# Token mixing of a hybrid layer: products of two heads side by side, TensorE's order by hand, two mLSTM blocks ahead of the attention queries

## The chip, the cores and the metric

The kernel runs on one core of one Trainium2 chip. The metric is the device time of one execution in microseconds (us), the median of three runs. A core has five engines, each with its own list of instructions in a fixed order: TensorE (PE: matrix products and transposes; PEld is its loading of weights), VectorE (DVE), ScalarE (ACT), GpSimd (POOL) and SyncE (SP, which issues transfers). They meet through semaphores.

## What is computed

One decoder layer in fp32 on 512 tokens of width 1024: token mixing, cross attention into 256 memory tokens, and a PEER feed-forward part (512 tokens x 8 heads x 16 experts, each a row of a table of 16384). The change touches only the token mixing:

```
proj = rmsnorm(h) @ w_in                      # -> mq, mk, mv, mo, mi, mf, aq, ak, av
# mLSTM, 4 heads, keys of 64, values of 128, in chunks; per head and chunk:
s    = (q k^T) * d                            # d: decays from the gates mi, mf, causal
num  = s v + w_inter * (C q);   den = sum(s) + w_inter * (n . q)
h    = num / max(|den|, exp(-m));  C = decay * C + sum(w v k^T);  n = decay * n + sum(w k)
hm   = sigmoid(mo) * rmsnorm_per_head(h)
# attention, 8 query heads on 2 key/value heads of 64, window 128, a sink logit per head:
p    = exp(scores - mx);  probs = p / (sum(p) + exp(sink - mx));  ha = probs @ av
h    = h + concat(hm, ha) @ w_out
```

## The kernel before

**Tiles.** The tokens stand in four blocks of 128 (`NB`). Dense products are made in three fp32r passes of a split operand: `whi`/`xhi` hold the value rounded to fp32r, `wlo`/`xlo` the rest, and each step is hi·hi, lo·hi, hi·lo (lines 946 to 948 with the weights on the stationary side, accumulator `acc_f`; lines 959 to 961 with the tokens stationary, accumulators `acc_o`, `acc_t`). The weights come as raw halves of 1 MB; ScalarE rounds them to `whi` and VectorE subtracts for `wlo` (lines 933 and 934, `load_w`, in as many pieces as `parts` says). `split_psum` does the same for results (lines 881 and 882). The small products of the mixing stage are plain fp32.

**Two shapes of small product use half of the array.** A product over the 64 channels of a head reads rows 0 to 63 or 64 to 127 ("64*128" in the trace): the mLSTM's `st` (line 212), the carried part of `num` (`num<-cst,qk`, line 253) and the scores `sp` (line 300). A product that makes 64 outputs fills columns 0 to 63 or 64 to 127 ("128*64"): `ds` (line 267, the update of the state `cst`) and `o_att` (line 334, the attention's output). An fp32 product stands in the trace as two records.

**Order of the stage, `front`.** After the dense projections of keys, values and gates, a loop over the four mLSTM heads makes `ab`, its exponential `dt` and `st`, and `pt` = `st` x `dt`. `wb` scales the queries in `qk`. The projection of the attention queries follows (`aq`, `acc_f0` to `acc_f3`, 96 passes). Then the string `MIX` interleaves three kinds of step over the blocks: `m` (a whole mLSTM block: keys `kw`, `num` of two tiles by row half, `den`, `hm`, the state update `ds`, the norm `rst`, four transposes `tp_hm` and their split), `s` (attention: scores of one half of the heads and their softmax, twice; then the transposes `tp_p`, the copies `pT` and the output of one half, twice) and `x` (the first 512 columns of `w_out` for one block, 24 `acc_o` products, and the residual). The softmax is eight exponentials on ScalarE per block (line 310) and scalings shared by VectorE (line 319) and ScalarE (line 317). The second half of `w_out` (`mix_out`) comes after the stage.

**What sets the order.** The string is only the order in which the program is traced. A scheduler with its own estimate of times then orders each engine's list, and moves instructions where it thinks that an operand is ready. Tiles of PSUM come in tags: `a` with two buffers, `b` with four, `d` with two; scores and output products share `b`, `num`, `st` and `ds` share `d`, transposes have `a`. A transfer of 8 MB of zeros (`wd<-zero`) is issued after `aq` is evacuated, and the loads of `w_out`'s first half are issued there too.

Of the kernel before, what the change touches and what calls it, by code (L numbers as in the profile page):

```python
# [21 lines left out]
P = 128  # L22
# [36 lines left out]
MIX = "s0 s1 m0 s0 s0 m1 s0 x0 s1 s2 s1 s1 s2 m2 s3 s2 s2 m3 s3 x1 x2 s3 s3 x3"  # L59
# [15 lines left out]
def front(c):  # L75
# [125 lines left out]
    for h in range(4):  # L201
        ab = ps.tile([P, 512], F32, tag="d", name="ab")
        T.matmul(ab, c.sel[:, h], raf, start=True, stop=False)
        T.matmul(ab, c.identb, c.cmask, start=False, stop=True)
        dt = c.np_.tile([P, D], F32, tag="xs", bufs=4, name="dt")[:, :S]
        for b in range(NB):
            A.activation(dt[:, b * P:(b + 1) * P], ab[:, b * P:(b + 1) * P], AF.Exp, bias=cols[:, b, h:h + 1])
# [14 lines left out]
    aq = fp.tile([P, 4, S], F32, name="aq")  # L222

    def evac_aq(j, acc):
        c.act_aq = A.copy(aq[:, j], acc)

    gemm_fm(c, [a["w_in_m"][3, hf] for hf in range(2)], evac_aq)

# [9 lines left out]
    hss = fp.tile([P, NB, 4], F32, name="hss")  # L238
    junk = fp.tile([P, P], F32, name="junk_h")
    def mlstm(b):  # L240
        t = slice(b * P, (b + 1) * P)
        hm = fp.tile([P, 4, P], F32, tag="hm", bufs=2, name="hm")
        if b < NB - 1:
            kw = make_kw(b)
        for hh in range(2):
            num = ps.tile([P, 512], F32, tag="d", name="num")
            n3 = num[:, :258].rearrange("p (h d) -> p h d", h=2)
            r = slice(64 * hh, 64 * hh + 64)
            for pr in range(2):
                h = 2 * pr + hh  # L250
                T.matmul(n3[:, pr], pt[h][:, t], vx[:, b, h], start=True, stop=(b == 0))
                if b:
                    T.matmul(n3[:, pr], qk[r, pr, t], cst[r, pr], start=False, stop=True)
            den = fp.tile([P, 2], F32, tag="den", bufs=2, name="den")
            A.activation(den, n3[:, :, P], AF.Abs)
            V.tensor_tensor(den, den, cols[:, b, 64 + hh:68 + hh:2], op=ALU.max)
            V.reciprocal(den, den)
            for pr in range(2):
                h = 2 * pr + hh
                V.tensor_scalar(hm[:, h], n3[:, pr, :P], den[:, pr:pr + 1], None, op0=ALU.mult)  # L260
                A.activation(junk, hm[:, h], AF.Square, accum_out=hss[:, b, h:h + 1])
        if b < NB - 1:
# [20 lines left out]
    def swa(b):  # L283
# [5 lines left out]
        scs = []  # L289
        for g in range(2):  # L290
            r = slice(64 * g, 64 * g + 64)
            snk = c.sinks[:, 4 * g:4 * g + 4]
            sc = fp.tile([P, 4, 256], F32, tag="sc", bufs=3, name="sc")
            mx = fp.tile([P, 4], F32, tag="mx", bufs=2, name="mx")
            for jj in range(2):
                sp = ps.tile([P, 512], F32, tag="b", name="sp")
                for j2 in range(2):
                    j = 2 * jj + j2
                    sl = sp[:, j2 * 256:j2 * 256 + nk]
                    T.matmul(sl, aq[r, j, t], kT[r, k0:k0 + nk], start=True, stop=True)  # L300
                    V.tensor_tensor_reduce(sc[:, j, :nk], sl, msk, 1.0, FMIN,
                                           op0=ALU.add, op1=ALU.max, accum_out=mx[:, j:j + 1])
            nm = fp.tile([P, 4], F32, tag="nm", bufs=2, name="nm")
            V.scalar_tensor_tensor(mx, mx, 0.125, snk, op0=ALU.mult, op1=ALU.max)
            V.tensor_scalar(nm, mx, -1.0, None, op0=ALU.mult)
            es = fp.tile([P, 4], F32, tag="es", bufs=2, name="es")
            V.tensor_tensor(es, snk, mx, op=ALU.subtract)
            den = fp.tile([P, 4], F32, tag="den4", bufs=2, name="den4")
            for j in range(4):
                A.activation(sc[:, j, :nk], sc[:, j, :nk], AF.Exp, bias=nm[:, j:j + 1], scale=0.125,  # L310
                             accum_out=den[:, j:j + 1])
            A.activation(es, es, AF.Exp)
            V.tensor_tensor(den, den, es, op=ALU.add)
            V.reciprocal(den, den)
            for j in range(4):
                if j % 2:
                    A.activation(sc[:, j, :nk], sc[:, j, :nk], AF.Copy, scale=den[:, j:j + 1])
                else:
                    V.tensor_scalar(sc[:, j, :nk], sc[:, j, :nk], den[:, j:j + 1], None, op0=ALU.mult)
            scs.append(sc)  # L320
            yield
        o = ps.tile([P, 512], F32, tag="b", name="o_att")
        for g, sc in enumerate(scs):
            pT = c.np_.tile([P, D], F32, tag="xs", bufs=4, name="pT")
            for kk in range(nkt):
                tp = ps.tile([P, 512], F32, tag="a", name="tp_p")
                for j in range(4):
                    T.transpose(tp[:, j * P:(j + 1) * P], sc[:, j, kk * P:(kk + 1) * P], ident)
                if kk:
                    A.copy(pT[:, 512:1024], tp)  # L330
                else:
                    V.tensor_copy(pT[:, 0:512], tp)
            for kk in range(nkt):
                T.matmul(o[64 * g:64 * g + 64], av[:, k0 // P + kk, 64 * g:64 * g + 64],  # L334
                         pT[:, kk * 512:(kk + 1) * 512], start=(kk == 0), stop=(kk == nkt - 1))
            if g == 0:
                yield
        split_psum(c, c.xhi[:, 4:8, t], c.xlo[:, 4:8, t], o.rearrange("p (h t) -> p h t", h=4))

# [6 lines left out]
    wo = [load_w(c, a["w_out"][0, hf], 512) for hf in range(2)]  # L346

    def mix0(b):
        acc = ps.tile([P, 512], F32, tag="b", name="acc_o")
        for hf in range(2):  # L350
            mm3_tm(c, acc, wo[hf], slice(0, 512), hf, b)
# [864 lines left out]
```

## Time and profile before

| | us |
|---|---|
| median of three runs | 1676.47 (1675.79 to 1678.25) |
| the profiled execution, its own time | 1678.69 |
| its span in the trace | 1676.9 |
| TensorE busy in the span | 1638.2 (98%) |
| VectorE busy | 1227.4 (73%) |
| ScalarE busy | 722.5 (43%) |
| TensorE's granted clock, mean | 0.986 |

The span is the time between the first and the last instruction of the profiled execution; the 1.8 us beside it are the start and the end of the run. A view by stages gives, for each stretch, how long each engine was busy and how many instructions it ran, the clock granted to TensorE as a share of full speed, and the load of the transfers. In a timeline, a row is a run of like instructions with its start; the start of the next row tells what the first one costs TensorE, since the records of products overlap (a record's length reaches into the next). The mixing stage lies between about 102 and 219 us of the span; the dense projection of the attention queries ends at 136.2 us.

### The profile page before, as it was taken

The numbers are of one execution on the slowest core, as the hardware profiler recorded it, in microseconds if no ns is written. First come the engines' busy times: TensorE is split into PE (matmuls) and PEld (weight loads), VectorE is DVE, ScalarE is ACT, GpSimd is POOL, SyncE is SP. The second block draws the span as 40 slices with busy tenths as digits, with TensorE's granted clock in tenths as the row PEclk, the third lists the DMA queues.
The fourth block names the chain that finished last, engine by engine and source line by source line (L and its number), as shares of the span: only waits on it lengthen the run. The fifth ranks groups of instructions, "written<-read, shape, count | busy, mean of one in ns | idle before, by whom it ended". The sixth has DMA issues, their size and how long they took to land.

```text
span 1676.9 us, 22996 instructions
## 1 busy us (share of the span) xinstructions
PE 1638.2 (98%) x8368; PEld 1427.2 (85%) x8368; DVE 1227.4 (73%) x2701; ACT 722.5 (43%) x1206; POOL 601.7 (36%) x427
## 2 busy tenths in 40 slices
PE   7999999999999999999999999999999999999987
PEld 5776579878999999899998988888888888888765
DVE  5535556465597888877887778878778888887985
ACT  5434544353354445578753333333333333333323
POOL 2000000000007878887423344434444344443620
PEclk9997999999999999999999999999999999999999
DMA  6236025215145444677999989898899899887992
GB/s 212 74 129 248 15 99 189 101 68 212 70 139 145 120 114 101 171 184 212 360 319 401 358 335 348 325 356 322 325 350 374 294 351 358 342 325 256 394 358 100
DMA packets 149105, 400.58 MB, mean 239 GB/s; under 512 B 28144, under 2 KB 62080, under 8 KB 136320
## 3 DMA queue, kind: packets, MB, share of 16 engines
q1 hardware_dynamic: 89232, 255.76, 41.6%
q0 software_dynamic: 55360, 134.32, 24.1%
q10 hardware_dynamic: 4400, 9.04, 1.5%
q8 instruction: 65, 1.06, 0.3%
q14 instruction: 48, 0.39, 0.1%
HBM read 356.28 MB, written 42.80 MB: 238 GB/s over the span
## 4 chain that ended last, share of the span: by engine, by line
PE 92%; DVE 3%; DMA 2%; issue 2%; ACT 1%; SPq 0%; DVEq 0%; POOLq 0%; POOL 0%; ACTq 0%
PE acc_d L782 10%; PE acc_d L780 10%; PE acc_d L781 10%; PE acc_u L847 9%; PE acc_u L846 9%; PE acc_u L848 9%; PE acc_f L946 4%; PE acc_f L948 4%; PE acc_f L947 4%; PE w L686 3%; PE acc_t L959 2%; PE acc_t L961 2%; PE acc_t L960 2%; PE sp L300 1%; PE o_att L334 1%
## 5 line engine op out<-in xcount | busy, mean ns | idle before, releaser
L780 PE MATMUL acc_d<-xhi,dh 128*128 128x384 f32 x1024 | 351.0, 343 | 4.6 <-ACT dh L731 3.6
L782 PE MATMUL acc_d<-xhi,dl 128*128 128x384 f32 x1024 | 345.7, 338 | 1.3 <-DVE dl L769 1.3
L781 PE MATMUL acc_d<-xlo,dh 128*128 128x384 f32 x1024 | 344.8, 337 | 0.0
L847 PE MATMUL acc_u<-ul,ch 128*128 128x512 f32 x762 | 299.2, 393 | 2.3 <-DVE ul L825 2.3
L848 PE MATMUL acc_u<-uh,cl 128*128 128x512 f32 x762 | 298.4, 392 | 0.0
L631 POOL DMA_INDIRECT wd<-gg,ei x128 | 234.4, 1831 | 148.4 <-DVE ei L625 87.3
L708 POOL DMA_INDIRECT rows<-in_down_r_dram,eidx x128 | 167.5, 1309 | 253.2 <-DVE dots L714 235.9
L708 POOL DMA_INDIRECT rows<-in_up_dram,eidx x128 | 175.5, 1371 | 214.3 <-DVE gacc L724 189.5
L834 ACT CAST ch<-cf 128x384 fp32r<-128x384 f32 x127 | 65.2, 514 | 395.1 <-issue 213.9
L846 PE MATMUL acc_u<-uh,ch 128*128 128x512 f32 x762 | 217.2, 392 | 3.6 <-ACT uh L731 3.6
L769 DVE TENSOR_TENSOR dl<-draw,dh 128x1024 fp32r<-128x1024 f32 x128 | 156.3, 1222 | 80.7 <-ACT dh L731 77.6
L731 ACT CAST dh<-draw 128x1024 fp32r<-128x1024 f32 x128 | 133.9, 1049 | 160.6 <-PE acc_d L781 137.0
L780 PEld LDWEIGHTS acc_d<-xhi,dh 128*128 128x128 f32 x1024 | 193.9, 189 | 9.5 <-ACT dh L731 3.9
L782 PEld LDWEIGHTS acc_d<-xhi,dl 128*128 128x128 f32 x1024 | 193.5, 189 | 5.5 <-DVE dl L769 2.4
L781 PEld LDWEIGHTS acc_d<-xlo,dh 128*128 128x128 f32 x1024 | 193.7, 189 | 4.0
L847 PEld LDWEIGHTS acc_u<-ul,ch 128*128 128x128 f32 x762 | 143.5, 188 | 33.8 <-DVE ul L825 4.8
L846 PEld LDWEIGHTS acc_u<-uh,ch 128*128 128x128 f32 x762 | 142.1, 188 | 31.0 <-ACT uh L731 4.5
L848 PEld LDWEIGHTS acc_u<-uh,cl 128*128 128x128 f32 x762 | 143.6, 188 | 28.7
L724 DVE SCALAR_TENSOR_TENSOR gacc<-rows,coef,gacc 128x1024 f32<-128x1024 f32 x127 | 162.8, 1282 | 0.4
L825 DVE TENSOR_TENSOR ul<-uraw,uh 128x1024 fp32r<-128x1024 f32 x127 | 154.7, 1223 | 2.9 <-ACT uh L731 2.1
L714 DVE CUSTOM_DVE_ANT_0 rows<-rows,xn 128x1024 f32<-128x1024 f32 x128 | 154.8, 1221 | 0.0
L835 DVE TENSOR_TENSOR cl<-cf,ch 128x384 fp32r<-128x384 f32 x127 | 70.7, 557 | 113.7 <-ACT ch L834 113.6
(333 smaller groups left out, 2667.6 us busy)
## 6 DMA issues: line engine op xcount, KB each, us to landing
draw<-in_down_t_dram SPq DMA_DIRECT2D x64, 1024.0 KB, 7.2
uraw<-in_up_dram SPq DMA_DIRECT2D x64, 1024.0 KB, 8.1
wt<-wd SPq DMA_DIRECT2D x96, 256.0 KB, 8.6
wd<-stg SPq DMA_DIRECT2D x8, 2048.0 KB, 11.8
gd<-gsp SPq DMA_DIRECT2D x17, 768.0 KB, 4.0
gsr<-gd SPq DMA_DIRECT2D x17, 768.0 KB, 10.6
wd<-zero ACTq DMA_DIRECT2D x1, 8192.0 KB, 27.7
raw<-in_w_pq_dram SPq DMA_DIRECT2D x8, 1024.0 KB, 5.3
```

The costliest lines, as they stand in the source:

```text
L631: i = G.indirect_dma_start(out=out, out_offset=bass.IndirectOffsetOnAxis(ap=ei[:, h, k:k + 1], axis=0), in_=c.gg[:, NG, hh, k:k + 1], in_o ...
L708: G.indirect_dma_start(out=r, out_offset=None, in_=src, in_offset=bass.IndirectOffsetOnAxis(ap=c.eidx[:, j:j + 1], axis=0))
L714: V.tensor_tensor_reduce(r, r, c.xn0, 1.0, 0.0, op0=ALU.mult, op1=ALU.add, accum_out=dots[:, j:j + 1])
L724: V.scalar_tensor_tensor(c.gacc, r, coef[:, j:j + 1], c.gacc, op0=ALU.mult, op1=ALU.add)
L769: c.dl = nc.vector.tensor_tensor(self.lo, raw, f32(self.hi), op=ALU.subtract)
L780: T.matmul(acc[:, :TD], self.hi[:, ks], c.xhi[:, k, NG * P:], start=(k == 0), stop=False)
L781: T.matmul(acc[:, :TD], self.hi[:, ks], c.xlo[:, k, NG * P:], start=False, stop=False)
L782: T.matmul(acc[:, :TD], self.lo[:, ks], c.xhi[:, k, NG * P:], start=False, stop=(k == KT - 1))
L825: V.tensor_tensor(lo, raw, f32(hi), op=ALU.subtract)
L846: T.matmul(acc[b][n], ch[:, t], hi[:, d], start=st, stop=False)
L847: T.matmul(acc[b][n], ch[:, t], lo[:, d], start=False, stop=False)
L848: T.matmul(acc[b][n], cl[:, t], hi[:, d], start=False, stop=sp)
```

## The change

Products that use different halves of the array stand next to each other in TensorE's list, one of each half: `st` of two heads, `num` of the two row halves, scores of the two key/value heads, `o_att` of the two column halves. For that the softmax takes all eight heads of a block at once (`sc` is 128 x 8 x 256, two buffers instead of three of half the size). An mLSTM block is a generator of two steps, `num` to `rst` and then the update of the state; its transposes and split are a third step of their own, `n` (`mlstm_out`), and `tp_hm` takes a buffer of tag `d`, `st` one of `a`. `hm` has three buffers. The first two mLSTM blocks are traced ahead of the projection of `aq`. `x` has two steps of 12 products. The first half of `w_out` is loaded in four parts each. The scheduler may no longer move TensorE's instructions of the loop: they stand as traced (`manual_schedule`); the other engines are still ordered by the scheduler.

```diff
-MIX = "s0 s1 m0 s0 s0 m1 s0 x0 s1 s2 s1 s1 s2 m2 s3 s2 s2 m3 s3 x1 x2 s3 s3 x3"
+MIX = ("s0 s0 n0 n1 s1 m2 s1 x0 s0 m2 s0 x1 x0 s2 s1 s2 s1 s3 m3 s1 s3 n2 x1 x2 s2 n3 s2 x3 s2 s3 x2 s3 s3 x3")
...
-        st = ps.tile([P, 512], F32, tag="d", name="st")
-        r = slice(64 * (h % 2), 64 * (h % 2) + 64)
+        sts = [ps.tile([P, 512], F32, tag="a", name="st") for _ in range(2)]
         for b in range(NB):
             t = slice(b * P, (b + 1) * P)
-            T.matmul(st[:, t], qk[r, 2 + h // 2, t], qk[r, h // 2, t], start=True, stop=True)
+            for hh in range(2):
+                r = slice(64 * hh, 64 * hh + 64)
+                T.matmul(sts[hh][:, t], qk[r, 2 + pr, t], qk[r, pr, t], start=True, stop=True)
...
-        hm = fp.tile([P, 4, P], F32, tag="hm", bufs=2, name="hm")
+        hm = hms[b] = fp.tile([P, 4, P], F32, tag="hm", bufs=3, name="hm")
...
+        for pr in range(2):
+            for hh in range(2):
+                T.matmul(n3[hh][:, pr], pt[2 * pr + hh][:, t], vx[:, b, 2 * pr + hh], start=True, stop=(b == 0))
+            for hh in range(2):
+                if b:
+                    r = slice(64 * hh, 64 * hh + 64)
+                    T.matmul(n3[hh][:, pr], qk[r, pr, t], cst[r, pr], start=False, stop=True)
...
+        rsqrt(c, rst[:, b], hss[:, b], 1.0 / P)
+        yield
         if b < NB - 1:
             for pr in range(2):
                 ds = ps.tile([P, 512], F32, tag="d", name="ds")
...
+    def mlstm_out(b):
+        t = slice(b * P, (b + 1) * P)
+        hm = hms.pop(b)
+        tp = ps.tile([P, 512], F32, tag="d", name="tp_hm")
...
+        sc = fp.tile([P, 8, 256], F32, tag="sc", bufs=2, name="sc")
+        mx = fp.tile([P, 8], F32, tag="mx", bufs=2, name="mx")
+        for jj in range(2):
+
+            sps = [ps.tile([P, 512], F32, tag="b", name="sp") for _ in gs]
+            for j2 in range(2):
+                for g, r in enumerate(gs):
+                    T.matmul(sps[g][:, j2 * 256:j2 * 256 + nk], aq[r, 2 * jj + j2, t], kT[r, k0:k0 + nk],
+                             start=True, stop=True)
...
+        for kk in range(nkt):
+            for g, r in enumerate(gs):
+                T.matmul(o[r], av[:, k0 // P + kk, r], pT[g][:, kk * 512:(kk + 1) * 512],
+                         start=(kk == 0), stop=(kk == nkt - 1))
...
+    ml = [mlstm(b) for b in range(NB)]
+    for b in range(2):
+        step(ml[b], 2)
+    aq = fp.tile([P, 4, S], F32, name="aq")
...
-    wo = [load_w(c, a["w_out"][0, hf], 512) for hf in range(2)]
+    wo = [load_w(c, a["w_out"][0, hf], 512, parts=4) for hf in range(2)]
...
+    with tc.manual_schedule(engines={mybir.EngineType.PE}):
+        for op in MIX.split():
+            k, b = op[0], int(op[1])
+            if k == "n":
+                mlstm_out(b)
+            else:
+                step(it[k][b], 1)
```

TensorE's list at the end of the `aq` projection, before (the names are output<-operands, with buffer numbers, and the columns of the result):

```order
L947 MATMUL acc_f3_844<-xlo_89,whi_900 128x512
L948 MATMUL acc_f3_844<-xhi_88,wlo_901 128x512
L300 MATMUL sp_979<-kT_346,aq_840 128x128
L233 MATMUL tp_k_1037<-ident_71,qk_499 128x128 x2
L219 MATMUL wb_836<-wi_472,selp_233 128x512
L251 MATMUL num_1041<-vx_235,pt0_784 128x129
L251 MATMUL num_1041<-vx_235,pt2_814 128x129
L300 MATMUL sp_984<-kT_346,aq_840 128x128
```

The same place in TensorE's list after:

```order
L970 MATMUL acc_f3_930<-xhi_88,whi_932 128x512
L233 MATMUL tp_k_846<-ident_71,qk_499 128x128 x2
L971 MATMUL acc_f3_930<-xlo_89,whi_932 128x512
L233 MATMUL tp_k_885<-ident_71,qk_499 128x128 x2
L972 MATMUL acc_f3_930<-xhi_88,wlo_933 128x512
L252 MATMUL num_850<-vx_235,pt0_797 128x129
L252 MATMUL num_850<-vx_235,pt2_827 128x129
L970 MATMUL acc_f3_930<-xhi_88,whi_932 128x512
```

The key transposes of mLSTM blocks 0 and 1 and block 0's `num`, which stood behind the projection among the first scores, stand inside it.

TensorE's list around block 2's `num`, before:

```order
L300 MATMUL sp_1217<-kT_346,aq_840 128x256
L300 MATMUL sp_1222<-kT_346,aq_840 128x256
L251 MATMUL num_1341<-vx_235,pt0_784 128x129
L253 MATMUL num_1341<-cst_957,qk_499 128x129
L251 MATMUL num_1341<-vx_235,pt2_814 128x129
L253 MATMUL num_1341<-cst_957,qk_499 128x129
L251 MATMUL num_1354<-vx_235,pt1_799 128x129
L253 MATMUL num_1354<-cst_957,qk_499 128x129
L251 MATMUL num_1354<-vx_235,pt3_829 128x129
L253 MATMUL num_1354<-cst_957,qk_499 128x129
L334 MATMUL o_att_1115<-pT_1179,av_347 64x512
```

The same block's `num` after (line 252 is the full-row part, line 256 the half-row part, line 305 the scores):

```order
L233 MATMUL tp_k_1163<-ident_71,qk_499 128x128 x2
L252 MATMUL num_1167<-vx_235,pt0_797 128x129
L252 MATMUL num_1168<-vx_235,pt1_799 128x129
L256 MATMUL num_1167<-cst_840,qk_499 128x129
L256 MATMUL num_1168<-cst_840,qk_499 128x129
L252 MATMUL num_1167<-vx_235,pt2_827 128x129
L252 MATMUL num_1168<-vx_235,pt3_829 128x129
L256 MATMUL num_1167<-cst_840,qk_499 128x129
L256 MATMUL num_1168<-cst_840,qk_499 128x129
L305 MATMUL sp_1196<-kT_346,aq_926 128x256
L305 MATMUL sp_1197<-kT_346,aq_926 128x256
```

Full-row and half-row products alternated one by one; now two of the one shape are followed by two of the other, and the two half-row products, as the two scores behind them, read different rows.

ScalarE's list between two blocks' softmax, before (line 310 is an exponential, line 330 a copy of `pT`, line 261 a square of the mLSTM's norm):

```order
L310 ACTIVATE sc_1215,den4_1232<-sc_1215,nm_1227 128x256 x2
L881 CAST xhi_88<-o_att_1115 128x4x128
L310 ACTIVATE sc_1215,den4_1232<-sc_1215,nm_1227 128x256 x2
L312 ACTIVATE es_1230<-es_1230 128x4
L261 ACTIVATE junk_h_959,hss_958<-hm_1335 128x128
L255 ACTIVATE den_1359<-num_1354 128x2
L330 COPY pT_1274<-tp_p_1281 128x512
```

ScalarE's list ahead of block 0's output product, after (line 322 is an exponential, line 328 a scaling, line 339 a copy of `pT`; `sc_1080` is block 0's, `sc_1149` block 1's):

```order
L322 ACTIVATE sc_1149,den8_1211<-sc_1149,nm_1206 128x256
L328 ACTIVATE sc_1080<-sc_1080,den8_1107 128x128 x4
L265 ACTIVATE junk_h_843,hss_841<-hm_1161 128x128
L322 ACTIVATE sc_1149,den8_1211<-sc_1149,nm_1206 128x256 x7
L265 ACTIVATE junk_h_843,hss_841<-hm_1161 128x128
L339 COPY pT_1245<-tp_p_1252 128x512
```

Block 1's eight exponentials stand ahead of the copy of block 0's transposed probabilities, seven of them behind the scaling of block 0; before, four stood between two such points.

## Rows read from the trace of the kernel before

**Rows 1.** Page, chain that ended last: shares of the span by engine.
```profile
PE 92%; DVE 3%; DMA 2%; issue 2%; ACT 1%; SPq 0%; DVEq 0%; POOLq 0%; POOL 0%; ACTq 0%
```

**Rows 2.** Stages: window, us, busy PE, PEld, DVE, ACT, POOL, PEclk, DMA, GB/s.
```profile
102.20:136.20 34.00, 34.00 (x143) 23.12 (x142) 8.62 (x9) 11.90 (x24) 0.00 (x0) 1.00 0.17 62
136.20:139.70 3.50, 3.50 (x17) 2.20 (x16) 2.25 (x6) 2.46 (x3) 0.00 (x0) 1.00 0.69 256
139.70:163.60 23.90, 23.09 (x73) 15.13 (x72) 15.68 (x79) 11.60 (x53) 2.03 (x2) 0.50 0.97 358
163.60:219.40 55.80, 55.71 (x249) 32.83 (x247) 31.76 (x120) 28.00 (x91) 2.26 (x3) 1.00 0.06 20
960.00:1600.00 640.00, 639.07 (x3068) 559.90 (x3067) 521.11 (x658) 222.19 (x307) 276.39 (x204) 1.00 0.90 338
```

**Rows 3.** Timeline of TensorE: start, us, line, names, tile, shape, records.
```profile
165.72 1.13 PE L300 MATMUL sp<-kT,aq 64*128 64x256 f32 x4
166.78 0.49 PE L251 MATMUL num<-vx,pt 128*128 128x129 f32 x2
...
173.87 0.70 PE L300 MATMUL sp<-kT,aq 64*128 64x256 f32 x2
174.50 0.50 PE L961 MATMUL acc_o<-whi,xlo 128*128 128x512 f32 x1
174.83 0.40 PE L959 MATMUL acc_o<-whi,xhi 128*128 128x512 f32 x1
175.07 0.40 PE L960 MATMUL acc_o<-wlo,xhi 128*128 128x512 f32 x1
...
178.03 0.70 PE L300 MATMUL sp<-kT,aq 64*128 64x256 f32 x4
178.66 1.07 PE L334 MATMUL o_att<-pT,av 128*64 128x512 f32 x2
...
184.18 0.66 PE L267 MATMUL ds<-vx,kw 128*64 128x129 f32 x8
184.77 0.66 PE L279 MATMUL tp_hm<-ident,hm 128*128 128x128 f32 x4
```

**Rows 4.** Timeline of TensorE, block 2's `num` and one output product.
```profile
167.20 0.49 PE L253 MATMUL num<-cst,qk 64*128 64x129 f32 x2
...
170.12 1.07 PE L334 MATMUL o_att<-pT,av 128*64 128x512 f32 x2
171.12 1.09 PE L328 MATMUL tp_p<-ident,sc 128*128 128x128 f32 x8
```

**Rows 5.** Stages, line 300 alone: PE, PEld, PEclk, DMA; then all three stages.
```profile
139.70:163.60 23.90, 6.79 (x22) 4.45 (x20) 0.50 0.97 358
...
sum 83.40, PE 17.41 PEld 10.47; mean PE 5.80 PEld 3.49
```

**Rows 6.** Timeline of TensorE, `st` of one mLSTM head.
```profile
130.39 1.16 PE L212 MATMUL st<-qk 64*128 64x128 f32 x8
```

**Rows 7.** Timeline of TensorE, four `num` records ahead of and behind the fall.
```profile
138.06 0.71 PE L251 MATMUL num<-vx,pt 128*128 128x129 f32 x4
...
139.78 1.23 PE L251 MATMUL num<-vx,pt 128*128 128x129 f32 x4
```

**Rows 8.** Groups, 136.2 to 219.4 us: count, busy us, mean ns, idle before.
```profile
L310 ACT ACTIVATE sc<-sc,nm 128x256 f32<-128x256 f32 x24 | 11.9, 496 | 5.8 <-DVE nm L305 5.8
...
L934 DVE TENSOR_TENSOR wlo<-raw,whi 128x2048 fp32r<-128x2048 f32 x2 | 4.6, 2286 | 0.8 <-ACT whi L933 0.8
...
L330 ACT COPY pT<-tp_p 128x512 f32<-128x512 f32 x6 | 3.5, 580 | 7.1 <-PE tp_p L328 7.1
...
L310 ACT ACTIVATE sc<-sc,nm 128x128 f32<-128x128 f32 x8 | 3.1, 386 | 0.0
```

**Rows 9.** Timeline: four passes on VectorE; TensorE's wait, [idle before <-releaser].
```profile
146.87 1.14 DVE L277 SCALAR_TENSOR_TENSOR hm<-hm,rst,gm 128x128 f32<-128x128 f32 x4 [0.38 <-POOL rst L877]
...
154.52 1.97 PE L334 MATMUL o_att<-pT,av 128*64 128x512 f32 x2 [0.78 <-DVE pT L332]
```

More of the change, by code (lines that the diff above doesn't have):

```diff
@@ L221, in front @@
         V.tensor_tensor(qk[:, pr], wb, qk[:, pr], op=ALU.mult)
[L222 to L227, printed above, removed]
     def make_kw(b):
@@ new lines, in swa @@
+        gs = [slice(0, 64), slice(64, 128)]
+        sc = fp.tile([P, 8, 256], F32, tag="sc", bufs=2, name="sc")
[6 more added lines that the diff above has]
+                             start=True, stop=True)
+            for j2 in range(2):
+                for g in range(2):
+                    h = 4 * g + 2 * jj + j2
+                    V.tensor_tensor_reduce(sc[:, h, :nk], sps[g][:, j2 * 256:j2 * 256 + nk], msk, 1.0, FMIN,
+                                           op0=ALU.add, op1=ALU.max, accum_out=mx[:, h:h + 1])
+            if jj == 0:
+                yield
@@ new lines, in swa @@
+        nm = fp.tile([P, 8], F32, tag="nm", bufs=2, name="nm")
+        V.scalar_tensor_tensor(mx, mx, 0.125, c.sinks, op0=ALU.mult, op1=ALU.max)
+        V.tensor_scalar(nm, mx, -1.0, None, op0=ALU.mult)
+        es = fp.tile([P, 8], F32, tag="es", bufs=2, name="es")
+        V.tensor_tensor(es, c.sinks, mx, op=ALU.subtract)
+        den = fp.tile([P, 8], F32, tag="den8", bufs=2, name="den8")
+        A.activation(es, es, AF.Exp)
+        for h in range(8):
+            A.activation(sc[:, h, :nk], sc[:, h, :nk], AF.Exp, bias=nm[:, h:h + 1], scale=0.125,
+                         accum_out=den[:, h:h + 1])
@@ new lines, in swa @@
+        V.tensor_tensor(den, den, es, op=ALU.add)
+        V.reciprocal(den, den)
+        for h in range(8):
+            if h % 2:
+                A.activation(sc[:, h, :nk], sc[:, h, :nk], AF.Copy, scale=den[:, h:h + 1])
+            else:
+                V.tensor_scalar(sc[:, h, :nk], sc[:, h, :nk], den[:, h:h + 1], None, op0=ALU.mult)
+        yield
+        pT = [c.np_.tile([P, D], F32, tag="xs", bufs=4, name="pT") for _ in gs]
+        for kk in range(nkt):
+            for g in range(2):
+                tp = ps.tile([P, 512], F32, tag="a", name="tp_p")
+                for j in range(4):
+                    T.transpose(tp[:, j * P:(j + 1) * P], sc[:, 4 * g + j, kk * P:(kk + 1) * P], ident)
+                if g:
+                    A.copy(pT[g][:, kk * 512:(kk + 1) * 512], tp)
+                else:
+                    V.tensor_copy(pT[g][:, kk * 512:(kk + 1) * 512], tp)
@@ L321, in swa @@
             yield
         o = ps.tile([P, 512], F32, tag="b", name="o_att")
[L323 to L337, printed above, removed]
@@ L340, in front, with evac_aq @@
+    aq = fp.tile([P, 4, S], F32, name="aq")
+    def evac_aq(j, acc):
+        c.act_aq = A.copy(aq[:, j], acc)
+    gemm_fm(c, [a["w_in_m"][3, hf] for hf in range(2)], evac_aq)
     with tc.issue_after(c.raw_dma.ins):
@@ L351, in mix0 @@
             mm3_tm(c, acc, wo[hf], slice(0, 512), hf, b)
+            if hf == 0:
+                yield
         resid(c, b, 0, acc)
-    sw = [swa(b) for b in range(NB)]
-    for op in MIX.split():
-        k, b = op[0], int(op[1])
-        if k == "s":
-            step(sw[b], 1)
-        elif k == "m":
-            mlstm(b)
-        else:
-            mix0(b)
+    it = {"s": [swa(b) for b in range(NB)], "x": [mix0(b) for b in range(NB)], "m": ml}
+    with tc.manual_schedule(engines={mybir.EngineType.PE}):
[3 more added lines that the diff above has]
+                mlstm_out(b)
+            else:
+                step(it[k][b], 1)
+    for k in it.values():
+        for g in k:
+            assert next(g, None) is None
 def mix_out(c):
```

77 lines of the change are left out of this document (22 added, 55 removed).

## Prediction

> **What bounds the kernel now.** I read first the chain of waits [rows 1]: 92% of the work that ended last is TensorE's. A microsecond taken from TensorE's own work is therefore a microsecond of the span, unless a wait takes its place. Then the stretch that the change touches, by stages [rows 2]: from 102.2 to 219.4 us TensorE idles for under 1 us in all. In that stretch the granted clock is 0.50 from 139.7 to 163.6 us, which is 1.2 instead of 2.4 GHz, and 1.00 on both sides. Before the fall TensorE had passed from the dense projection to small products; before it rose it ran `acc_o` products back to back. The rest of the kernel stands behind TensorE as well (639.07 of 640 us busy from 960 us on, last of rows 2), and its order is the same in both versions but for a few neighbours; so what the mixing stage gains by the start of `w_out`'s second half should arrive at the end. Last I read the spacing of the small products, from one start to the next.
>
> **Pairs.** A lone score product of 256 columns takes 0.63 us with the step into and out of its half-row shape (173.87 to 174.50); two on the same half take 1.06 (165.72 to 166.78), so 0.43 each and 0.20 for the step. Four records, two products of different halves that happen to stand together, take 0.63 again (178.03 to 178.66) [rows 3]: the second costs nothing. The same holds for column halves: `ds`, four products of 129 columns in two pairs, takes 0.59 us (184.18 to 184.77), while one `num` product in a shape of its own takes 0.42 (166.78 to 167.20) [rows 3, 4]. The sum at full clock:
> - Attention output, 14 products of 1.00 us each (170.12 to 171.12 [rows 4]), become 7 pairs: 14.0 to 7.0, saves 7.0.
> - Scores: line 300 sums to 17.41 us, of which 6.79 at half clock are 3.4 at full [rows 5]: 14.0 us. After, eight groups of two pairs, six at 1.13 as the row at 165.72 and two at 0.70: 8.2. Saves 5.8, less 0.3 for one group that `ds` splits: 5.5.
> - `num`: today each block from 1 on alternates full and half rows, 8 products in 3.34 us (166.78 to 170.12 [rows 3, 4]). New order per two heads: two full-row products (0.42 + 0.22) and a pair (0.42), 2.1 us a block. Saves 1.2 in blocks 2 and 3, about 0.5 in block 1, whose products are scattered: 2.9.
> - `st`: 4 groups of 1.1 us [rows 6] become 2; one product of the second stands out of turn (0.2). Saves 2.0.
> - Added: mLSTM blocks 0 and 1 are cut into pieces between `acc_f` products, some four extra steps of 0.2: 0.8.
>
> Sum **16.6 us** saved. The lower bound, if only row halves paired, is 9.6; from above nothing more, as the pairs cannot cost less than one product.
>
> One rule of the Trainium skill (TensorE: Matmul & The Clock Gate, Part 3, The mechanism) speaks against a part: weights are loaded during a running product only when the row group differs. Column halves share all rows, so by it the attention output would keep its 14.0 us and the sum be 9.6. The `ds` rows disagree, 0.59 us for four.
>
> **The half-speed stretch.** 23.9 us with 23.09 us busy [rows 2] would be 11.5 us at full clock, so it costs 11.5 (the same four `num` records take 0.71 us before the fall and 1.23 after it [rows 7]). The new order also enters a stretch of small products behind the projection, so a fall is likely again; it is shorter, and runs of 12 and 24 `acc_o` stand in it. Bounds: all 11.5 back, or nothing.
>
> **New waits.** At present the half speed and the slow order hide the other engines: one wait of 0.78 us [rows 9]. With TensorE's order fixed and 16.6 us less of it, these show, worked out at full clock:
> - Behind the projection VectorE holds four parts of a weight's low half (2.29 [rows 8] in sum) and some 16 short passes (over `hm`, `cst` and scores, and two low halves) at 0.29 each, as four in 1.14 us [rows 9]: 6.9 us. TensorE has scores 0.6, `ds` 0.6, scores 0.4, eight transposes 1.2, scores 1.1, `tp_k` 0.4: 4.3. Wait 2.6, up to 3.5 as links alternate.
> - Block 0's transposes need eight exponentials of 0.39 [rows 8], the reciprocal and a scaling, some 4 us after VectorE's part of 3.4; TensorE has `num` 2.1, scores 0.9 and 12 `acc_o` of 0.24 (174.83 to 175.07 [rows 3]), 5.9. Wait 1.5.
> - ScalarE's list has seven exponentials of block 1 (0.50 [rows 8], 3.5 us) ahead of the copy of `pT` (0.58) that block 0's output product waits for; TensorE has 1.0 us between. Wait 3.1.
> - Near the end two `acc_o` products need a low half that is queued on VectorE behind four scalings of about 0.3 and behind 2.29 of a `wlo` with a `pT` copy. Waits 1.6 and 2.2.
>
> Sum about **11 to 12 us**, 8 of them where the clock is likely low, and there they hide it or are hidden by it. From both sides: 4, if the engines run ahead as today, to 16, if every link adds 0.2.
>
> **Costed at nothing.** The move of blocks 0 and 1 into the projection: VectorE is busy 8.62 and ScalarE 11.90 of 34.0 us there [rows 2], so their 8 us fit. `w_out` in four parts: its loads are issued long before the 8 MB of zeros; if not, x0's first half would wait. Merged eight-wide softmax steps take some 2 us from VectorE that it partly idles. At the very end SyncE's queue has one `hb` load ahead of the last but one `uraw`: 0 to +2.
>
> **Sum.** The likeliest case has the clock fall again and waits and low clock overlap: 16.6 + 11.5 + 0.8 saved, 12 of waits and 2 to 3 of low clock not covered by them come in: **-14.5 us**. Against the profiled execution, 1678.69 us with a span of 1676.9, that is 1664.2; the median of 1676.47 lies 2.2 lower, so 1662.
>
> **Rivals.**
> - *The clock stays up and VectorE keeps pace*: no half-speed stretch and waits of 6: -16.6 - 11.5 - 0.8 + 6 = -22.9, 1653.6. For it: from 163.6 us on the clock stayed at 1.00 through 55.8 us of small and dense products mixed [rows 2]. Against: the links in which TensorE idles. Chance 0.08.
> - *Column halves do not overlap* (the rule above): -14.5 + 7.0 = -7.5, 1669. Against: `ds` [rows 3]. Chance 0.04.
> - *The change does not do what it says*, pairs run one after the other since the second product waits for its own semaphores: 16.6 comes back, about 8 of the waits go: -5.9, 1670.6. The pair at 178.03 [rows 3] speaks against it. With a wash of other terms to no change: chance 0.06.
> - *Slower*: the clock stays at 1.2 GHz through the whole mixing stage, because a fixed order with waits never lets it rise. Some 51 us of TensorE's work from the end of the projection to `w_out`'s second half would take 102 and hide all waits: at about 243 instead of 219.4, +24, 1700. It decides once the half-speed stretch passes about 53 us (23.9 and twice 14.5). Against: dense `acc_o` ended it in 23.9 us before, and runs of 24 stand in the new order. Chance 0.05.
>
> **Numbers.** The forecast has 0.77. Its own range comes from waits of 4 to 16 and a low clock that costs 0 to 5: 1656 to 1667; taking in the first rival below and the third above, 1653 to 1671. About 0.2% (3.4 us) is what a measurement here can tell from no change: faster 0.90 (the third's 0.06 splits into 0.01, 0.04 and 0.01), same 0.04, slower 0.06.
>
> **What would show it.** Right: `sp`, `st` and output products start in twos a few ns apart; line 346 takes half of 14.0; TensorE idles 6 to 14 us between the projection and `w_out`'s second half, most before one output product and the late `acc_o`; that second half starts near 205 instead of 219.4. Wrong: output products 1 us apart, a half-speed stretch over 30 us, or idle time over 16.

## The result and the profile after

The changed kernel takes 1663.22 us (median of 5 runs, 1660.87 to 1664.09) against 1675.79 us of the kernel before in the same series: a ratio of 0.9923 (95% interval 0.9908 to 0.9939), 12.6 us less. The forecast was 1662, -14.5 us against the profiled execution. The profiled execution has a span of 1661.6 us against 1676.9, 15.3 less; that of the kernel before took 1678.69 us, 2.9 above the median of the series, so a sum over the two traces comes out larger than the medians say.

The gain is complete where the prediction looked for it. The first `acc_t` product of `w_out`'s second half starts at 204.06 us instead of 219.4, and the last product of the program is 15.3 us earlier as well. The view by stages of the changed kernel, from the point where the mixing stage begins to that product (us, busy time and instructions of PE, PEld, DVE, ACT, POOL, then granted clock, DMA share, GB/s), answers to [rows 2]:

```profile
102.20:139.70 37.50, 37.25 (x179) 24.96 (x178) 15.48 (x39) 15.22 (x45) 1.02 (x1) 1.00 0.17 56
139.70:144.34 4.64, 3.33 (x30) 2.26 (x30) 4.02 (x18) 3.24 (x8) 1.01 (x1) 1.00 0.76 281
144.34:147.75 3.41, 3.41 (x15) 2.25 (x16) 3.41 (x15) 0.73 (x2) 0.00 (x0) 0.50 1.04 384
147.75:161.41 13.66, 10.03 (x58) 6.14 (x57) 9.06 (x48) 11.50 (x53) 1.12 (x1) 1.00 1.03 378
161.41:164.82 3.41, 3.41 (x8) 2.70 (x9) 1.65 (x5) 0.93 (x3) 0.00 (x0) 0.50 1.05 408
164.82:204.06 39.24, 33.88 (x189) 23.10 (x187) 22.52 (x79) 22.85 (x67) 2.12 (x3) 1.00 0.17 62
```

Three sums come out of such rows. TensorE's **work** at full clock is its busy time, half of it where the clock is 0.50: 37.25 + 3.33 + 1.70 + 10.03 + 1.70 + 33.88 = 87.9 us. The **half clock** costs the other halves, 3.4 us. The rest is **waiting**, 10.6 us. The same sums of [rows 2] are 104.8, 11.5 and 0.9 us. So the change took 16.9 us of work and 8.1 us of half clock, and gave back 9.7 us as waits: -15.3.

TensorE's timeline shows the pairs (start, us, line, names, tile, shape, records). The start of the next row is the end of the cost:

```profile
104.54 1.16 PE L218 MATMUL st<-qk 64*128 64x128 f32 x16
...
148.29 0.49 PE L256 MATMUL num<-cst,qk 64*128 64x129 f32 x4
148.71 0.71 PE L252 MATMUL num<-vx,pt 128*128 128x129 f32 x4
149.36 0.49 PE L256 MATMUL num<-cst,qk 64*128 64x129 f32 x4
149.68 1.03 PE L305 MATMUL sp<-kT,aq 64*128 64x256 f32 x8
150.64 0.50 PE L983 MATMUL acc_o<-whi,xhi 128*128 128x512 f32 x1
...
156.58 1.02 PE L346 MATMUL o_att<-pT,av 128*64 128x512 f32 x2
160.32 1.07 PE L346 MATMUL o_att<-pT,av 128*64 128x512 f32 x2 [2.72 <-ACT pT L339]
...
176.04 1.94 PE L346 MATMUL o_att<-pT,av 128*64 128x512 f32 x8
177.91 1.14 PE L305 MATMUL sp<-kT,aq 64*128 64x256 f32 x8
```

Sixteen `st` records take the 1.16 us that eight took [rows 6]. Eight score records, four products, take 0.96 us here and 1.06 to 1.07 in three later groups, where four records of one half took 1.06 [rows 3]. Four output products take 1.87 us, so a pair 0.94, where one took 1.00 [rows 4]. Block 0's two output products are the exception: they stand next to each other in the list but start 3.7 us apart (156.58 and 160.32), since the second waits for its `pT`. And four half-row records of `num` take 0.42, what two took.

What TensorE waited for between 139 and 204 us (waiter <- releaser: us in total, times, longest), where before one wait of 0.78 us stood [rows 9]:

```profile
PE acc_o L985 <- DVE xlo L906: 3.7, 2, 2.2
PE o_att L346 <- ACT pT L339: 2.7, 1, 2.7
PE tp_hm L287 <- ACT sc L328: 1.7, 1, 1.7
PE tp_hm L287 <- DVE cst L277: 0.6, 2, 0.4
PE tp_p L337 <- ACT sc L328: 0.5, 1, 0.5
PE tp_p L337 <- DVE sc L330: 0.4, 1, 0.4
PE sp L305 <- ACT aq L356: 0.4, 1, 0.4
PE sp L305 <- DVE mx L310: 0.3, 1, 0.3
```

The 2.7 us are the copy of `pT` behind block 1's exponentials. ScalarE's timeline ends with the last of seven exponentials and one square ahead of it:

```profile
158.92 0.49 ACT L322 ACTIVATE sc<-sc,nm 128x256 f32<-128x256 f32 x1
159.32 0.19 ACT L322 ACTIVATION_READ_ACCUMULATOR sc<-sc,nm 128x1 f32 x1
159.41 0.29 ACT L265 ACTIVATE junk_h<-hm 128x128 f32<-128x128 f32 x1
159.61 0.19 ACT L265 ACTIVATION_READ_ACCUMULATOR junk_h<-hm 128x1 f32 x1
159.71 0.56 ACT L339 COPY pT<-tp_p 128x512 f32<-128x512 f32 x1
```

The chain of the page moved accordingly, from 92% TensorE [rows 1] to 89%:

```profile
PE 89%; DVE 5%; issue 3%; ACT 2%; DMA 1%; POOL 0%; DVEq 0%; POOLq 0%; ACTq 0%
```

### The profile page after: what moved, and what is told of

It is laid out like the page before. It is cut to its first block, busy times and chain, and to the rows that moved or that the text cites. A ratio compares the mean times of both kernels' runs of the same rounds, so it can differ in the third digit from the quotient of the medians.

```text
span 1661.6 us, 22993 instructions
## 1 busy us (share of the span) xinstructions
PE 1613.3 (97%) x8367; PEld 1415.6 (85%) x8368; DVE 1224.1 (74%) x2686; ACT 722.1 (43%) x1209; POOL 599.1 (36%) x427
## 3 DMA queue, kind: packets, MB, share of 16 engines
q8 instruction: 65, 1.06, 0.3%
## 4 chain that ended last, share of the span: by engine, by line
PE 89%; DVE 5%; issue 3%; ACT 2%; DMA 1%; POOL 0%; DVEq 0%; POOLq 0%; ACTq 0%
PE acc_d L806 10%; PE acc_d L805 10%; PE acc_d L804 10%; PE acc_u L871 9%; PE acc_u L872 9%; PE acc_u L870 9%; PE acc_f L970 4%; PE acc_f L972 4%; PE acc_f L971 4%; PE w L710 3%; PE acc_t L984 2%; PE acc_t L985 2%; PE acc_t L983 2%; DVE ul L849 1%; PE s L550 1%
## 5 line engine op out<-in xcount | busy, mean ns | idle before, releaser
L655 POOL DMA_INDIRECT wd<-gg,ei x128 | 232.5, 1816 | 147.8 <-DVE ei L649 87.3
L732 POOL DMA_INDIRECT rows<-in_up_dram,eidx x128 | 175.8, 1373 | 212.7 <-DVE gacc L748 187.8
L804 PEld LDWEIGHTS acc_d<-xhi,dh 128*128 128x128 f32 x1024 | 194.2, 190 | 10.5 <-ACT dh L755 5.0
```

The lines of the kernel that those rows point to most:

```text
L655: i = G.indirect_dma_start(out=out, out_offset=bass.IndirectOffsetOnAxis(ap=ei[:, h, k:k + 1], axis=0), in_=c.gg[:, NG, hh, k:k + 1], in_o ...
L732: G.indirect_dma_start(out=r, out_offset=None, in_=src, in_offset=bass.IndirectOffsetOnAxis(ap=c.eidx[:, j:j + 1], axis=0))
L804: T.matmul(acc[:, :TD], self.hi[:, ks], c.xhi[:, k, NG * P:], start=(k == 0), stop=False)
```

## The experiments

The theory is the prediction's sum: pairs take TensorE's work away, and what comes next are waits on VectorE and ScalarE. The rivals are that the order by hand and the early blocks carry the gain, that single terms are hidden, and, for the half clock, three causes: lone small products, the place of the two mLSTM blocks, and a lack of dense products. All edits are to the changed kernel except where the kernel before is named. The table gives the three sums of each profiled execution, made like those above, from 102.2 us to the first `acc_t` of `w_out`'s second half, and the ratio of the times to the kernel before. "Low behind aq" is the time at clock 0.50 behind the `aq` projection and ahead of that product. The clock in the projection itself differs from run to run, so the ratios, not one trace, decide small differences. A ratio difference of 0.001 is 1.7 us.

| kernel | acc_t starts | work | half clock | waits | low behind aq | ratio (95%) |
|---|---|---|---|---|---|---|
| before | 219.4 | 104.8 | 11.5 | 0.9 | 23.9 | 1 |
| changed | 204.1 | 87.9 | 3.4 | 10.6 | 6.8 | 0.9923 (0.9908-0.9939) |
| e1 no pairs | 212.7 | 100.2 | 5.1 | 5.2 | 3.4 | 0.9962 (0.9948-0.9976) |
| e2 no output pairs | 204.0 | 91.8 | 3.4 | 6.6 | 6.8 | 0.9915 (0.9899-0.9932) |
| e3 no score pairs | 206.9 | 93.6 | 3.4 | 7.7 | 6.8 | 0.9932 (0.9915-0.9948) |
| e4 scheduler's order | 207.5 | 97.0 | 3.4 | 4.9 | 0 | 0.9944 (0.9928-0.9961) |
| b1 kernel before, blocks ahead of aq | 239.4 | 103.2 | 25.4 | 8.7 | 13.7 | 1.0137 (1.0107-1.0167) |
| e5 blocks behind aq | 212.6 | 86.3 | 10.5 | 13.5 | 20.5 | 0.9967 (0.9951-0.9982) |
| e10 both undone | 222.4 | 97.4 | 15.9 | 6.9 | 27.3 | 1.0031 (1.0020-1.0041) |
| e6 w_out in whole halves | 205.7 | 88.2 | 5.1 | 10.2 | 6.8 | 0.9909 (0.9891-0.9927) |
| e11 dense products late | 211.8 | 87.4 | 10.1 | 12.0 | 6.8 | 0.9938 (0.9920-0.9956) |
| e7 pT on VectorE | 202.7 | 87.3 | 5.1 | 8.1 | 6.8 | 0.9926 (0.9904-0.9948) |
| e9 and w_out 2 in parts | 201.5 | 88.3 | 3.4 | 7.5 | 0 | 0.9906 (0.9884-0.9928) |
| e12 and the split first | 197.8 | 88.2 | 1.5 | 5.9 | 3.4 | 0.9879 (0.9862-0.9895) |

### Nothing side by side (e1)

The edit, abridged (`...` stands for what is left out):

```
-  r = slice(64 * hh, 64 * hh + 64);  T.matmul(sts[hh]..., qk[r...]...)      # st, and num's half-row part
+  r = slice(0, 64)
-  T.matmul(sps[g]..., aq[r, ...], kT[r, ...])
+  T.matmul(sps[g]..., aq[gs[0], ...], kT[gs[0], ...])
-  T.matmul(o[r], av[:, k0 // P + kk, r], pT[g]...)
+  T.matmul(o, av[:, k0 // P + kk], pT[g]...)
```

> The changed kernel with nothing side by side, all else in the same place: scores, st and the carried part of num of both heads read the first half's rows (so the second head's values are not the reference's), and the attention's output product makes all 128 columns and adds both halves into one tile. Theory, the pairs carry the gain: output products 7.5 to 12-14 us, scores 8.6 to 13, half-row part of num 2.9 to 4.7, st 2.2 to 4.3, so 13 to 16 us more of TensorE's work, of which the waits (10 us) hide 3 to 6: the second half of w_out starts at 212 to 217 instead of 204.1 us, time 1671 to 1678, near before. Rival, the order and the early blocks carry the gain: start at 204 to 207, time within 3 us of the changed kernel. Rival on the clock: if lone small products make the long half-speed stretch, it grows from 6.8 to over 20 us and the start lies beyond 219.

Work rose by 12.3 us, less than the 13 to 16 expected. By line and at full clock the scores take 5.9 us more, the output products 3.8, `st` 1.6 and `num`'s half-row part 1.1; an output product of full width costs 0.91 us (four in 3.64, below). The start of `acc_t` is at the lower end of the theory's range, the time (1669.42) 1.6 us below it. In this trace `acc_t` starts 8.7 us later than in the changed kernel: 12.3 of work and 1.7 of half clock, less 5.4 of waits. Up to the projection's end the clock differs from execution to execution, and this one (1672.16 us) was 2.7 us above the median of its kernel; by the ratios the pairs are worth 6.5 us. The rival on the clock falls plainly. In two of its stages the clock is 1.00 for 54.6 us on end and 0.50 for 3.4; the last product of the projection starts at 144.9, so 21 us of the first stage are lone small products with 12 `acc_o` among them:

```profile
111.69:166.30 54.61, 51.17 (x251) 35.73 (x249) 27.52 (x111) 24.87 (x93) 2.92 (x3) 1.00 0.43 157
166.30:169.72 3.42, 3.42 (x9) 2.33 (x8) 1.99 (x6) 1.44 (x4) 0.23 (x1) 0.50 1.05 411
```

### One kind of pair taken out (e2, e3)

e2 has the last edit above alone, e3 the one on `sps`.

> Only the attention's output products are taken out of their pairs: each makes all 128 columns, and both halves add into one tile (the attention's output is not the reference's). Theory: 14 products of 0.86 us, 12.0 instead of 7.5, so +4.5, of which late waits hide at most 2: the second half of w_out starts at 206.5 to 208.6, time +2.5 to +4.5. Rival, that term is hidden behind the waits: start within 1 us of 204.1.

> Only the scores are taken out of their pairs: both key/value heads read the first half's rows (the second head's scores are not the reference's), same order. Theory: scores 8.6 to 13-14 us, of which 1 to 2 are hidden behind VectorE's reductions after the projection: start of the second half of w_out at 207 to 209, time +3 to +5. Rival, the reductions on VectorE hide all of it: within 1 us.

The rival took e2: work +3.9, waits -4.0, start 204.0. Two pairs of output products, now one after the other, take 3.64 us instead of 1.87, and the transposes behind them wait no more; TensorE's timeline and its waits show it:

```profile
175.93 3.70 PE L346 MATMUL o_att<-pT,av 128*128 128x512 f32 x8
179.57 1.13 PE L305 MATMUL sp<-kT,aq 64*128 64x256 f32 x8
180.63 0.66 PE L287 MATMUL tp_hm<-ident,hm 128*128 128x128 f32 x4
```

```profile
PE o_att L346 <- ACT pT L339: 2.5, 1, 2.5
PE acc_o L985 <- DVE xlo L906: 1.8, 2, 1.1
```

The wait of 1.7 us of `tp_hm` on a ScalarE scaling is gone and that on `xlo` is halved. As the changed kernel stands, the pairs of output products are worth nothing alone (the ratio says the same, 0.9915): they bring TensorE to points where its operands are not ready. In e3 a group of four scores takes 1.82 us (149.26 to 151.08) instead of 0.96; work +5.7, waits -2.9, start 206.9. That is the theory's lower end; the time, 1665.34 us, is 2.1 above the changed kernel, less than the 3 to 5 expected, and the intervals of the two ratios overlap.

```profile
149.26 1.89 PE L305 MATMUL sp<-kT,aq 64*128 64x256 f32 x8
151.08 0.50 PE L983 MATMUL acc_o<-whi,xhi 128*128 128x512 f32 x1
```

### The scheduler's order instead of the one by hand (e4)

```
-    with tc.manual_schedule(engines={mybir.EngineType.PE}):
```

> The changed kernel without the order by hand: the scheduler places TensorE's instructions of the mixing loop. By its list 14 of 32 scores stand in pairs instead of 30, 6 of 14 output products instead of 14, 2 of 12 half-row products of num instead of 10. Theory: 8 x 0.43 + 4 x 1.0 + 4 x 0.4 = 9 us more of TensorE's work, and 4 to 8 us less of waits: the second half of w_out starts at 205 to 209, time +1 to +5. Rival, the fixed order costs more than the broken pairs: start at 196 to 203. Rival, the scheduler's order brings the long half-speed stretch back: start beyond 212.

As the theory says: work +9.1 (9 expected), waits -5.7, start 207.5, 1667.29 us. In the traces the order by hand is worth some 3.4 us, all of it by keeping the pairs together; what it adds is waits. By the ratios it is 3.5 us, with intervals that overlap a little. The long half-clock stretch did not come back, though the scheduler placed the products again; blocks 0 and 1 still stood inside the projection.

### The two mLSTM blocks behind the projection (b1, e5, e10)

b1 was the kernel before with `for b in range(2): mlstm(b)` moved ahead of `gemm_fm` of `aq` (so `m0` and `m1` leave `MIX`) and nothing else.

> The kernel before with one part of the change alone: mLSTM blocks 0 and 1 are traced ahead of the aq projection. No product gets a partner, the scheduler keeps TensorE's order. If the place of the two blocks is what shortens the half-speed stretch (the first dense acc_o then stand 10 small products behind the projection), the stretch of 23.9 us shrinks to 3 to 10 us, and the time falls by 4 to 8 us to 1668 to 1672. Rival, the stretch is made by lone small products: it stays at 17 us or more, and the time within 2 us of before.

The edit was wrong for its purpose: `mlstm` ends with a split that writes `xhi` and `xlo`, which the projection reads. So the projection read other values for their tokens and stood behind both blocks: its first product starts at 144.77 us, its last at 169.1 instead of 135.9.

```profile
104.86:149.23 44.37, 40.65 (x114) 24.79 (x115) 18.56 (x57) 11.96 (x49) 3.04 (x3) 0.50 0.07 24
149.23:173.12 23.89, 22.87 (x103) 18.07 (x101) 5.37 (x10) 6.06 (x6) 0.00 (x0) 1.00 0.24 86
173.12:186.78 13.66, 10.08 (x24) 5.90 (x25) 6.73 (x39) 7.62 (x33) 0.00 (x0) 0.50 1.03 368
```

```profile
144.77 2.08 PE L949 MATMUL acc_f<-xhi,whi 128*128 128x512 f32 x4 [0.68 <-ACT xhi L884]
```

Of the 44 us at half clock all but the last 4.5 lie ahead of the projection, where TensorE ran `ab`, `st`, `wb` and the mLSTM's products with no dense ones among them. Behind the projection the clock was low for 13.7 us, between the 3 to 10 of the theory and the 17 of the rival. So the run (1699.64 us) does not answer its question: the blocks stand ahead of the projection instead of inside it, and the longest low stretch lies there with them. It does show why the change has `mlstm_out` as a step of its own behind the projection. Whether the early blocks alone help the kernel before was not tried again; the other direction was, abridged:

```
     ml = [mlstm(b) for b in range(NB)]
-    for b in range(2):
-        step(ml[b], 2)
     ...
     gemm_fm(c, [a["w_in_m"][3, hf] for hf in range(2)], evac_aq)
+    for b in range(2):
+        step(ml[b], 2)
```

> The changed kernel with blocks 0 and 1 traced behind the aq projection again, pairs and the order by hand kept. Theory: about 8 us of work on VectorE and ScalarE leave the projection and stand in front of the scores and exponentials, so TensorE's waits grow by 3 to 8 us: the second half of w_out starts at 206 to 212 instead of 204.1. If the place of the blocks makes the half-speed stretch, that also grows from 6.8 to over 13 us. Rival, the work fits behind the projection as well: start within 1.5 us.

> Both parts undone in the changed kernel: nothing side by side, as in the first run (the same values are not the reference's), and blocks 0 and 1 behind the projection; TensorE's order by hand stays. Theory, two separate gains: no pairs cost 8.7 at the start of the second half of w_out, blocks behind 8.5, both together 15 to 19: start at 219 to 223, time 1674 to 1680; the half-speed stretch is long (over 13 us), since the place of the blocks makes it. Rival, lone products only fill the waits that the late blocks make: start at 213 to 217.

e10 has this edit and that of e1. Both came out near the theory: starts 212.6 (0.6 above its range) and 222.4, and the half-clock stretch behind the projection is long again, with pairs and without. This does not rest on two traces alone: the mean granted clock over all executions of each kernel is 0.993 in the changed one and 0.992 in e1, 0.987 in e5 (ten executions) and 0.984 in e10 (nine); the other kernels with the blocks inside the projection lie between 0.990 and 0.993. The stages of e5 and of e10:

```profile
142.64:159.70 17.06, 14.26 (x60) 9.58 (x61) 10.05 (x43) 8.45 (x40) 2.03 (x2) 0.50 1.04 379
```

```profile
146.69:174.00 27.31, 24.94 (x77) 17.99 (x77) 13.99 (x62) 12.50 (x59) 3.04 (x3) 0.50 0.71 262
```

In e5 TensorE also waits for what block 0 and 1 need on VectorE:

```profile
PE ds L273 <- DVE hm L264: 3.2, 2, 2.9
PE ds L273 <- DVE den L260: 1.9, 1, 1.9
```

So in the traces the place of the blocks is worth 8.5 us at `acc_t` with pairs, 9.6 without (222.4 less 212.7). Pairs are worth 8.7 with the blocks ahead and 9.8 with them behind. Both undone cost 18.3, a little more than 8.5 + 8.7. By the ratios the place is worth 7.4 us, the pairs 6.5 and both together 18.1; the intervals are too wide (each difference has some 3 to 4 us either way) to say whether the two add up or help each other. What is left with both undone, the order by hand with its merged softmax, is slower than the kernel before (ratio 1.0031; time 1682.92, above the range expected).

### Dense products late (e11) and whole halves of w_out (e6)

```
-MIX = ("s0 s0 n0 n1 s1 m2 s1 x0 s0 m2 s0 x1 x0 s2 ...
+MIX = ("s0 s0 n0 n1 s1 m2 s1 s0 m2 s0 x0 x1 x0 s2 ...
```

> The changed kernel with the first 12 acc_o products of block 0 moved from behind block 2's scores to behind block 0's output product, so the stretch of small products behind the projection has no dense ones within it. Theory, dense products keep or bring back the clock: half-speed time in the stage grows from 6.8 to over 13 us. And the transposes of block 0 lose their cover of 2.8 us: start at 206 to 208 without a change of the clock, 209 to 213 with it. Rival on the clock: it stays at 3 to 10 us.

In this trace the rival on the clock holds: 6.8 us low behind the projection, as in the changed kernel, though no dense product stands between the projection and 167.75 us. In this execution the clock was low for 13.65 us within the projection itself, ahead of anything that was moved; without its 6.8 us the start would lie near 205. Three stages of it:

```profile
113.32:126.97 13.65, 13.65 (x38) 7.90 (x38) 2.81 (x6) 1.14 (x4) 0.00 (x0) 0.50 0.01 1
...
154.27:161.10 6.83, 3.22 (x26) 2.22 (x24) 5.94 (x35) 4.75 (x27) 0.00 (x0) 1.00 1.01 346
161.10:164.52 3.42, 3.14 (x16) 2.50 (x17) 1.32 (x3) 3.42 (x15) 0.00 (x0) 0.50 1.05 410
```

The middle row shows the lost cover: TensorE is busy for 3.22 of 6.83 us. Block 0's transposes wait 3.9 us instead of 0.9, but the copy of `pT` behind them only 1.5 instead of 2.7, and all waits together grow by 1.4. The time, 1668.22 us (1666.08 to 1672.69), is 2.5 us above the changed kernel by the ratios, whose intervals overlap. The mean clock of its four executions lies between 0.986 (the profiled one) and 0.992, so whether the move has a part in the low clock ahead of it is left open.

e6 drops `parts=4` in the loads of the first half of `w_out`.

> The changed kernel with the first half of w_out loaded and rounded in whole halves instead of four parts each. Theory: the parts were costed at nothing; whole low halves of 2.29 us stand in front of scores or num on VectorE behind the projection: start at 203.5 to 206.5. Rival, the first x0 waits for its weights, as the first 12 products then need a whole half: start at 207 or later.

Start 205.7, of which 1.7 us is more half clock; work and waits are as before within 0.4 us and the ratio is that of the changed kernel. The parts cost and bring nothing that can be measured.

### The waits taken away (e7, e9, e12)

```
-                if g:
+                if g and b:                        # e7, e9, e12: block 0's second copy of pT on VectorE
                     A.copy(pT[g]...)
...
-    gemm_tm(c, [c.a["w_out"][1, hf] for hf in range(2)], ...)
+    gemm_tm(c, [load_w(c, c.a["w_out"][1, hf], 512, parts=4) for hf in range(2)], ...)      # e9, e12
...
+        with tc.high_priority(offset=HP):          # e12: split of tp_hm in mlstm_out
             split_psum(c, c.xhi[:, 0:4, t], c.xlo[:, 0:4, t], ...)
```

> The changed kernel with block 0's second copy of pT on VectorE instead of behind seven exponentials on ScalarE. Theory: the wait of 2.7 us at 160 us goes; VectorE and ScalarE then stand nearer to the later waits, which take 0 to 2 of it back: the second half of w_out starts at 201.5 to 203, time -1 to -2.7. Rival, all is given back by the waits at 191 and 199 us: start 204.

> As the run before, and the second half of w_out is loaded in four parts, so that its low half begins on VectorE 1.4 us earlier, ahead of the attention's low half. Theory: the wait of 2.2 us at 199.6 shrinks to about 0.8: start at 200 to 202, time 1658.5 to 1661.5. Rival: ScalarE and VectorE take up the smaller steps in the same time, no gain over the run before.

> As the run with pT on VectorE and w_out's second half in parts, and the split of the mLSTM's transposes is given precedence, so that on VectorE it stands behind one scaling of block 3 instead of four. Theory: the wait of 1.6 us at 190 shrinks by 0.6 to 0.9: start of the second half of w_out at 200.5 to 201, time 1659 to 1661.5, ratio to before 0.988 to 0.991. Rival: the three scalings behind it delay block 3's transposes by as much: start 201.5.

Each wait goes or shrinks where it was attacked. In e7 the 2.7 us on `pT` are gone and the start is 1.4 earlier, with 1.7 us more half clock in that execution; in the times (1664.38) no gain can be told. e9 starts at 201.5 and takes 1661.5 us, the upper end of its range; by the ratio this cannot be told from the changed kernel. In its trace the wait near 199 us fell from 2.15 to 0.96 us, that near 190 stayed at 1.51:

```profile
190.03 0.50 PE L985 MATMUL acc_o<-whi,xlo 128*128 128x512 f32 x1 [1.51 <-DVE xlo L906]
...
197.08 0.50 PE L985 MATMUL acc_o<-whi,xlo 128*128 128x512 f32 x1 [0.96 <-DVE xlo L906]
```

e12 starts at 197.8, 1.9 us of it less half clock than the changed kernel, and takes 1657.33 us, ratio 0.9879 (0.9862 to 0.9895); start and time are below what was expected. Its interval lies below that of the changed kernel, so it is faster than both versions. All waits on `xlo` fell from 3.7 us in the changed kernel to 2.0, and the one at 190 us, which the precedence was for, from 1.51 to 0.73. VectorE's timeline shows the low half behind one scaling instead of four:

```profile
PE acc_o L986 <- DVE xlo L907: 2.0, 3, 1.0
```

```profile
186.31 0.50 PE L986 MATMUL acc_o<-whi,xlo 128*128 128x512 f32 x1 [0.73 <-DVE xlo L907]
```

```profile
185.30 0.36 DVE L331 TENSOR_SCALAR sc<-sc,den 128x256 f32<-128x256 f32 x1
185.56 0.69 DVE L907 TENSOR_TENSOR xlo<-tp_hm,xhi 128x512 fp32r<-128x512 f32 x1
186.16 0.87 DVE L331 TENSOR_SCALAR sc<-sc,den 128x256 f32<-128x256 f32 x3
```

## Why the prediction was right, and where not

- **Pairs, 16.6 us of TensorE's work.** Measured 16.9, and right term by term. By line, at full clock and up to `acc_t`: output products 6.8 (7.0 forecast; one of the fourteen stands behind that start before, two do after), scores 5.5 (5.5), `num` 3.0 (2.9), `st` 2.3 (2.0). Output pairs were put at 1.00 and took 0.94 to 1.01, but only six of the seven are side by side; groups of scores were put at 1.13 and took 0.96 to 1.07. e1 brings back 12.3 of the 16.9; the rest comes with what e1 keeps, output products without a change of shape and `num` grouped by shape. The Trainium skill's rule on weight loads (TensorE: Matmul & The Clock Gate, Part 3, The mechanism), from which the prediction drew that column halves would gain nothing, does not reach that far: four output products in 1.87 us are overlapped. The Trainium skill gives column tiles a gain too (TensorE: Matmul & The Clock Gate, Measured speedup vs the span model: 2.38 times for three), and the trace agrees that they gain: two output products that took 1.00 us each, with the step into their shape, take 0.94 together.
- **New waits, 11 to 12 us.** Measured 10.6, and mostly at the places named: the copy of `pT` 2.7 (3.1 forecast), the two low halves near the end 3.7 together (1.6 and 2.2), block 0's transposes 0.9 (1.5), behind the projection 1.3 (2.6 to 3.5). One was not foreseen, 1.7 us of `tp_hm` at 180.7.
- **Half clock.** 11.5 us were to come back but for 2 to 3; 8.1 did, so 3.4 remained. The size was right, but by luck, as the reason does not hold. "Runs of 12 and 24 `acc_o` stand in it" was given; in e11 the first 12 are gone from the stretch and the low time behind the projection stays at 6.8, and e1 has lone products and no long low stretch. The place of blocks 0 and 1 decides in the changed kernel: with them behind the projection 20.5 and 27.3 us are low (23.9 before), with their products inside it 0 to 6.8 in all ten kernels that have them there. In b1, where they stand ahead of it, 13.7 us behind it and some 40 ahead are low.
- **The step that was mis-sized** is thus the move of the blocks: the prediction charged it 0.8 us for extra steps, called the rest free and booked its gain under the clock. Undoing it costs 8.5 us in the traces (7.4 by the ratios), about 7 of half clock, 1.7 of them ahead of the projection's end, and 3 of waits, less 1.6 of work.
- **The sum.** -14.5 forecast, -15.3 measured at `acc_t` and at the end of the traces, -12.6 by the medians of one series. The terms agree, but a term's work is not what its removal costs: in the traces 2.8 us for the scores (work 5.7), nothing for the output products (3.9), 8.7 for all four kinds (12.3), since from about half to all of what is taken from TensorE is given back as waits. "A microsecond taken from TensorE's own work is therefore a microsecond of the span, unless a wait takes its place" holds by its second half.
- **The rivals.** Waits of 6 with the clock up came near in e12, a kernel with three more edits (waits 5.9, half clock 1.5, start 197.8 where -22.9 would be 196.5) but not in the changed kernel. A clock that stays low did not happen; e10 is the nearest, 27.3 us.

## What to carry to other kernels

Where TensorE bounds a stage, half-row and half-column products of two heads beside each other can cost what one costs, as they do here, and their saving can be counted from the spacing of starts before the change. Then list at once which queue is late next, since here it took back half or more: a copy behind another block's exponentials, and low halves behind scalings that nobody waits for yet; precedence for one such short step took 0.8 us off the wait it was for (e12). Small products that need nothing of a dense projection are worth trying inside it: here that paid about as much as all the pairs.

## What the runs showed that was not expected

The long half-clock stretch is tied neither to waits nor to lone products. Before, the clock fell at 139.7 us with TensorE busy 23.09 of 23.90 us in the stretch [rows 2], and in e10 24.94 of 27.31; in the changed kernel TensorE waits for 3.6 of 13.66 us (147.75 to 161.41) at clock 1.00, and the clock is low only for 3.41 us on either side of it. In the kernel before, e5, e10 and b1, which have the long low stretches, the products of the first mLSTM blocks stand outside the dense projection; what in them goes with the low clock was not separated. The clock within the projection differs between kernels with the same list there, from no low stretch (changed) to 13.65 us (e11), which moves a single execution by up to 7 us.
